# LogSumExp over rows: the second pass on another queue, the range check in two parts, two loads in quarters

## The chip, the cores and the metric

The kernel runs on one core of one Trainium2 chip. The metric is the device time of one execution in microseconds. Nine runs of the kernel before gave a median of 165.54 us, from 165.21 to 165.82.

## The reference

For every row of `x`, of shape 32 x 512 x 1024 in float32, the reference computes the logarithm of the sum of exponentials, made safe by the row's maximum:

```python
max_x = np.max(x, axis=-1, keepdims=True)
return (max_x.squeeze(-1) + np.log(np.sum(np.exp(x - max_x), axis=-1))).astype(np.float32)
```

The input is drawn from a standard normal distribution. That makes 16,384 rows of 4 KB, 67.11 MB to read and 64 KB to write.

## The kernel before

The 16,384 rows are laid over 128 partitions: partition p holds the 128 consecutive rows from 128 p on, so a row index `c` from 0 to 127 names one row on every partition. Neighbouring partitions lie 512 KB apart in memory. The kernel gambles that no maximum is needed: it takes exp, sum and logarithm directly, checks at the end that all sums were in a safe range, and only if one was not does it run a second pass that subtracts the maximum.

**The first pass.** Seventeen loads, listed as strings in `loads` (L42), go through the SyncE (SP) queue into `ring`, a buffer of 48 rows per partition that is filled round and round. A load moves between 16 rows and 1 row per partition; the sizes fall towards the end. The string says how the rows are then summed: `R8` is an exp over eight rows on ScalarE (L92) and one reduction on VectorE (L99); `A` is an exp on ScalarE whose own accumulator gives the sum (L90); `T` is an exp on ScalarE and then one VectorE instruction per row that adds the row's halves and accumulates (L104). The sums go to `sumexp`, one column per row index. The logarithm is taken in two parts: the first 104 columns in the middle of the stream (L119), the last 24 at the end (L121). Then SP writes `res` out (L122).

**The range check.** After the stream, VectorE clamps 127 columns of `sumexp` into 1e-15 to 1e15 (L127) and compares them with the originals, with an accumulated count of the unequal ones in `bad` (L131). The 128th row, the last to arrive, is treated apart: the maximum of the first 256 elements of its input is taken (L136) and compared with -34 (L137), and its sum itself enters the total. Three tiny matmuls add everything over the partitions into one number `count` in PSUM (L135, L140, L141), and `fine` is whether that number is below 1e15 (L143).

**The branch and the end.** `values_load` (L144) has SP, ScalarE and VectorE each load `fine` into a register and branch on it (L148). In the untaken case each engine brings its semaphores up to what the second pass would have made of them and jumps to the end. There SP waits for every semaphore that the program used, one or two at a time, and drains. All engines then meet at a barrier that GpSimd gathers and releases.

**What sets the order.** Each engine works its instructions in program order. A framework assigns the waits: every DMA takes the next of eight hardware semaphores in turn, and waits that the program declares unneeded are left out. The closing waits of SP name these semaphores in a list; the one of the output DMA stands first in the kernel before.

The second pass (L149 to L160) runs on SP for the loads and the store, on VectorE and ScalarE for the computation. With the given input it is not executed.

Of the kernel before, what the change touches and what calls it, by code (L numbers as in the profile page):

```python
# [9 lines left out]
LOW, HIGH = 1e-15, 1e15  # L10
LOG_LOW = -34.0


@with_exitstack
def kernel(
    ctx: ExitStack,
    tc: tile.TileContext,
    x: bass.AP,
    out: bass.AP,
):  # L20
    nc = tc.nc
    P = nc.NUM_PARTITIONS
    fp32 = mybir.dt.float32
    i32 = mybir.dt.int32
    AF = mybir.ActivationFunctionType
    AX = mybir.AxisListType
    ALU = mybir.AluOpType

    x_flat = x.flatten_outer_dims()
    n, d = x_flat.shape  # L30
    assert n % P == 0
    NC = n // P
    H = d // 2

    x_rows = x_flat.rearrange("(p c) d -> p c d", p=P)
    out_view = out.rearrange("a b -> (a b)").rearrange("(p c) -> p c", p=P)

    RING = 48
    loads = [  # L42
        "R8 R8", "R8 R8", "R8 R8", "R7 R6 A A", "R6 R5 A A A", "R5 R4 A", "R5 R4", "R5 T3",
        "R3 A A A", "R3 A", "R2 T2", "R3", "R1 A", "T2", "T1", "A", "A",
    ]
    loads = [[(op[0], int(op[1:] or 1)) for op in load.split()] for load in loads]
    assert sum(s for ops in loads for _, s in ops) == NC
    ENGINES = [mybir.EngineType.SP, mybir.EngineType.Activation, mybir.EngineType.DVE]
    EARLY = 104
    LAST = NC - 1  # L50

    big = ctx.enter_context(tc.tile_pool(name="big", bufs=1))
    stats = ctx.enter_context(tc.tile_pool(name="stats", bufs=1))
    psum = ctx.enter_context(tc.tile_pool(name="psum", bufs=1, space=bass.MemoryType.PSUM))

    ring = big.tile([P, RING, d], fp32, name="ring")
    sumexp = stats.tile([P, NC], fp32, name="sumexp")
    res = stats.tile([P, NC], fp32, name="res")
    clamped = stats.tile([P, NC], fp32, name="clamped")
    bad = stats.tile([P, 3], fp32, name="bad")  # L60
    fine = stats.tile([1, 1], i32, name="fine")
    far = stats.tile([P, 1], fp32, name="far")
    ones = stats.tile([P, 1], fp32, name="ones")
    last_exp = psum.tile([P, 1, d], fp32, name="last_exp")
    count = psum.tile([1, 1], fp32, name="count")

    nc.scalar.preload_act_table_set("natural_log_exp_and_others")  # L67
    nc.vector.memset(ones, 1.0)  # L68
    nc.vector.memset(far, 100 * HIGH)

    def load(p0, c0, size):
        return nc.sync.dma_start(out=ring[:, p0 : p0 + size, :], in_=x_rows[:, c0 : c0 + size, :])  # L72

    def without_wait(ins, group, reason):

        tc.declare_no_dep(ins.ins, group=group, reason=reason)

    c = 0
    p = 0
    for ops in loads:  # L80
        size = sum(s for _, s in ops)
        if p + size > RING:
            p = 0
        dma = load(p, c, size).ins
        for how, s in ops:
            v = ring[:, p : p + s, :]
            sums = sumexp[:, c : c + s]
            if how == "A":
                o = v if c < LAST else last_exp
                exp = nc.scalar.activation(out=o, in_=v, func=AF.Exp, accum_out=sums)  # L90
            else:
                exp = nc.scalar.activation(out=v, in_=v, func=AF.Exp)  # L92
            without_wait(exp, "loads", "the slot's earlier users came before this load")
            without_wait(exp, "exps", "the slot's earlier users came before this load")
            without_wait(exp, "sums", "the slot's earlier users came before this load")
            tc.add_to_no_dep_group("exps", exp.ins)
            added = []
            if how == "R":
                added = [nc.vector.reduce_sum(out=sums, in_=v, axis=AX.X)]  # L99
            elif how == "T":  # L100
                for r in range(s):
                    lo = ring[:, p + r, 0:H]
                    added.append(
                        nc.vector.scalar_tensor_tensor(  # L104
                            out=lo, in0=lo, scalar=1.0, in1=ring[:, p + r, H:d],
                            op0=ALU.mult, op1=ALU.add, accum_out=sums[:, r : r + 1],
                        )
                    )
            for add in added:
                tc.declare_no_dep(add.ins, dma, reason="ScalarE has waited for it")  # L110
                without_wait(add, "loads", "they came before this one")
            for add in added:
                tc.add_to_no_dep_group("sums", add.ins)
            c += s
            p += s
            last_row = v
        tc.add_to_no_dep_group("loads", dma)
        if c == EARLY + 14:
            nc.scalar.activation(out=res[:, 0:EARLY], in_=sumexp[:, 0:EARLY], func=AF.Ln)  # L119

    nc.scalar.activation(out=res[:, EARLY:NC], in_=sumexp[:, EARLY:NC], func=AF.Ln)  # L121
    nc.sync.dma_start(out=out_view, in_=res)  # L122

    nc.vector.tensor_scalar(  # L127
        out=clamped[:, 0:LAST], in0=sumexp[:, 0:LAST],
        scalar1=LOW, scalar2=HIGH, op0=ALU.max, op1=ALU.min,
    )  # L130
    nc.vector.scalar_tensor_tensor(  # L131
        out=clamped[:, 0:LAST], in0=clamped[:, 0:LAST], scalar=0.0, in1=sumexp[:, 0:LAST],
        op0=ALU.bypass, op1=ALU.not_equal, accum_out=bad[:, 0:1],
    )
    nc.tensor.matmul(count, lhsT=bad[:, 0:1], rhs=far, start=True, stop=False)  # L135
    nc.vector.reduce_max(out=bad[:, 2:3], in_=last_row[:, 0, 0 : d // 4], axis=AX.X)  # L136
    nc.vector.tensor_scalar(  # L137
        out=bad[:, 1:2], in0=bad[:, 2:3], scalar1=LOG_LOW, scalar2=None, op0=ALU.is_lt
    )
    nc.tensor.matmul(count, lhsT=bad[:, 1:2], rhs=far, start=False, stop=False)  # L140
    nc.tensor.matmul(count, lhsT=sumexp[:, LAST:NC], rhs=ones, start=False, stop=True)  # L141

    nc.vector.tensor_scalar(out=fine, in0=count, scalar1=HIGH, scalar2=None, op0=ALU.is_lt)  # L143
    all_fine = nc.values_load(  # L144
        fine[0:1, 0:1], engines=ENGINES, min_val=0, max_val=1,
        skip_runtime_bounds_check_because="a truth value",
    )
    with tc.If(all_fine < 1, preferred_fallthrough_block=False):  # L148
        for c0 in range(0, NC, RING):  # L149
            s = min(RING, NC - c0)  # L150
            v = ring[:, 0:s, :]
            neg = clamped[:, c0 : c0 + s]
            load(0, c0, s)
            nc.vector.tensor_reduce(out=neg, in_=v, op=ALU.max, axis=AX.X, negate=True)
            nc.vector.tensor_add(out=v, in0=v, in1=neg[:, :, None].to_broadcast([P, s, d]))
            nc.scalar.activation(out=v, in_=v, func=AF.Exp)
            nc.vector.reduce_sum(out=sumexp[:, c0 : c0 + s], in_=v, axis=AX.X)
        nc.scalar.activation(out=res, in_=sumexp, func=AF.Ln)
        nc.vector.tensor_sub(out=res, in0=res, in1=clamped)
        nc.sync.dma_start(out=out_view, in_=res)  # L160


# [28 lines left out]
```

## Time and profile before

| what | value |
|---|---|
| median of nine runs | 165.54 us (165.21 to 165.82) |
| profiled execution, its own time | 165.34 us |
| its span | 163.5 us |
| VectorE busy | 122.2 us, 75% |
| ScalarE busy | 116.7 us, 71% |
| TensorE busy | 0.4 us |
| load queue, share of the 16 DMA engines | 95.9% |
| mean transfer rate over the span | 411 GB/s |

The span is the time from the first to the last instruction of the program; the execution's own time is 1.8 us longer. PE is the TensorE matmul, PEld its weight load, DVE VectorE, ACT ScalarE, POOL GpSimd and SP SyncE; a q behind a name means the sequencer or queue of that engine. Branches, semaphore waits and register loads are not counted as busy and appear only when a source line is asked for.

### The profile page before, as it was taken

The numbers are of one execution on the slowest core, as the hardware profiler recorded it, in microseconds if no ns is written. First come the engines' busy times: TensorE is split into PE (matmuls) and PEld (weight loads), VectorE is DVE, ScalarE is ACT, GpSimd is POOL, SyncE is SP. The second block draws the span as 40 slices with busy tenths as digits, with TensorE's granted clock in tenths as the row PEclk, the third lists the DMA queues.
The fourth block names the chain that finished last, engine by engine and source line by source line (L and its number), as shares of the span: only waits on it lengthen the run. The fifth ranks groups of instructions, "written<-read, shape, count | busy, mean of one in ns | idle before, by whom it ended". The sixth has DMA issues, their size and how long they took to land.

```text
span 163.5 us, 205 instructions
## 1 busy us (share of the span) xinstructions
PE 0.4 (0%) x6; PEld 0.2 (0%) x6; DVE 122.2 (75%) x44; ACT 116.7 (71%) x53; POOL 0.2 (0%) x4
## 2 busy tenths in 40 slices
PE   0000000000000000000000000000000000000001
PEld 0000000000000000000000000000000000000000
DVE  0000000699968999499999995999998999979893
ACT  3000039990699708995499839999969599999992
POOL 0000000000000000000000000000000000000000
DMA  7979988998997998899999999999999999999970
GB/s 256 497 337 449 513 385 385 513 417 353 513 449 321 513 482 376 361 481 481 449 435 407 435 391 431 411 409 433 433 449 425 411 445 419 421 427 417 411 281 20
DMA packets 2594, 67.19 MB, mean 411 GB/s; under 512 B 288, under 2 KB 416, under 8 KB 800
## 3 DMA queue, kind: packets, MB, share of 16 engines
q1 hardware_dynamic: 2592, 67.18, 95.9%
q14 instruction: 2, 0.02, 0.0%
HBM read 67.11 MB, written 0.07 MB: 411 GB/s over the span
## 4 chain that ended last, share of the span: by engine, by line
DMA 63%; DVE 22%; ACT 12%; issue 1%; SPq 0%; PE 0%; DVEq 0%
DMA ring<-in_x_dram 63%; DVE sumexp L99 20%; ACT ring L92 12%; DVE ring L104 1%; SPq L72 0%; DVE bad L136 0%; DVE clamped L127 0%; PE count L140 0%; DVE bad L137 0%; DVE clamped L131 0%; DVE fine L143 0%; PE count L141 0%; DVEq L127 0%
## 5 line engine op out<-in xcount | busy, mean ns | idle before, releaser
L99 DVE TENSOR_REDUCE sumexp<-ring 128x8 f32<-128x8192 f32 (+7 forms) x20 | 116.2, 5854 | 37.7 <-ACT ring L92 37.6
L92 ACT ACTIVATE ring<-ring 128x8192 f32<-128x8192 f32 (+7 forms) x24 | 101.7, 4283 | 43.1 <-DMA ring<-in_x_dram 43.1
L90 ACT ACTIVATE ring<-ring 128x1024 f32<-128x1024 f32 x12 | 12.5, 1039 | 0.0
L104 DVE SCALAR_TENSOR_TENSOR ring<-ring 128x512 f32<-128x512 f32 x8 | 5.1, 684 | 0.0
L90 ACT ACTIVATION_READ_ACCUMULATOR ring<-ring 128x1 f32 x12 | 2.2, 186 | 0.0
L67 ACT ACT_TABLE_LOAD x1 | 1.3, 1283 | 0.7 <-PEq L175 0.7
L90 ACT ACTIVATE last_exp<-ring 128x1024 f32<-128x1024 f32 x1 | 1.0, 1014 | 0.0
L68 DVE MEMSET ones<- 128x1 f32 x1 | 0.1, 59 | 0.8 <-PEq L175 0.8
L104 DVE DVE_READ_ACCUMULATOR ring<-ring 128x1 f32 x8 | 0.7, 82 | 0.0
L135 PE MATMUL count<-far,bad 128*1 128x1 f32 x2 | 0.2, 164 | 160.3 <-DVE clamped L131 160.3
L136 DVE TENSOR_REDUCE bad<-ring 128x1 f32<-128x256 f32 x1 | 0.4, 415 | 0.0
L143 DVE TENSOR_SCALAR fine<-count 1x1 int32<-1x1 f32 x1 | 0.1, 147 | 0.3 <-PE count L141 0.3
L131 DVE SCALAR_TENSOR_TENSOR clamped<-clamped,sumexp 128x127 f32<-128x127 f32 x1 | 0.3, 291 | 0.0
L127 DVE TENSOR_SCALAR clamped<-sumexp 128x127 f32<-128x127 f32 x1 | 0.2, 227 | 0.1
L135 PEld LDWEIGHTS count<-far,bad 128*1 128x1 f32 x2 | 0.1, 80 | 160.3 <-DVE clamped L131 160.3
L119 ACT ACTIVATE res<-sumexp 128x104 f32<-128x104 f32 x1 | 0.3, 273 | 0.0
L121 ACT ACTIVATE res<-sumexp 128x24 f32<-128x24 f32 x1 | 0.2, 223 | 0.0
L140 PE MATMUL count<-far,bad 128*1 128x1 f32 x2 | 0.2, 164 | 0.3 <-DVE bad L137 0.3
L141 PE MATMUL count<-ones,sumexp 128*1 128x1 f32 x2 | 0.2, 164 | 0.0
L90 ACT ACTIVATION_READ_ACCUMULATOR last_exp<-ring 128x1 f32 x1 | 0.2, 186 | 0.0
L137 DVE TENSOR_SCALAR bad<-bad 128x1 f32<-128x1 f32 x1 | 0.2, 154 | 0.0
L141 PEld LDWEIGHTS count<-ones,sumexp 128*1 128x1 f32 x2 | 0.1, 81 | 0.0
(7 smaller groups left out, 0.6 us busy)
## 6 DMA issues: line engine op xcount, KB each, us to landing
ring<-in_x_dram SPq DMA_DIRECT2D x1, 7680.0 KB, 32.5
ring<-in_x_dram SPq DMA_DIRECT2D x1, 7168.0 KB, 30.1
ring<-in_x_dram SPq DMA_DIRECT2D x1, 5120.0 KB, 31.4
ring<-in_x_dram SPq DMA_DIRECT2D x1, 4608.0 KB, 33.7
ring<-in_x_dram SPq DMA_DIRECT2D x1, 4096.0 KB, 29.3
ring<-in_x_dram SPq DMA_DIRECT2D x2, 2048.0 KB, 32.7
ring<-in_x_dram SPq DMA_DIRECT2D x1, 3072.0 KB, 36.3
ring<-in_x_dram SPq DMA_DIRECT2D x2, 1024.0 KB, 38.8
```

The costliest lines, as they stand in the source:

```text
L67: nc.scalar.preload_act_table_set("natural_log_exp_and_others")
L90: exp = nc.scalar.activation(out=o, in_=v, func=AF.Exp, accum_out=sums)
L92: exp = nc.scalar.activation(out=v, in_=v, func=AF.Exp)
L99: added = [nc.vector.reduce_sum(out=sums, in_=v, axis=AX.X)]
L104: nc.vector.scalar_tensor_tensor(out=lo, in0=lo, scalar=1.0, in1=ring[:, p + r, H:d], op0=ALU.mult, op1=ALU.add, accum_out=sums[:, r : r + 1],
L119: nc.scalar.activation(out=res[:, 0:EARLY], in_=sumexp[:, 0:EARLY], func=AF.Ln)
L121: nc.scalar.activation(out=res[:, EARLY:NC], in_=sumexp[:, EARLY:NC], func=AF.Ln)
L127: nc.vector.tensor_scalar(out=clamped[:, 0:LAST], in0=sumexp[:, 0:LAST], scalar1=LOW, scalar2=HIGH, op0=ALU.max, op1=ALU.min,)
L131: nc.vector.scalar_tensor_tensor(out=clamped[:, 0:LAST], in0=clamped[:, 0:LAST], scalar=0.0, in1=sumexp[:, 0:LAST], op0=ALU.bypass, op1=AL ...
L135: nc.tensor.matmul(count, lhsT=bad[:, 0:1], rhs=far, start=True, stop=False)
L136: nc.vector.reduce_max(out=bad[:, 2:3], in_=last_row[:, 0, 0 : d // 4], axis=AX.X)
L141: nc.tensor.matmul(count, lhsT=sumexp[:, LAST:NC], rhs=ones, start=False, stop=True)
```

## The change

The change has three parts.

First, SP no longer loads `fine` and does not branch; only ScalarE and VectorE do. The second pass is put into a critical section, in which the framework places no waits of its own and the program uses two semaphores, `landed` and `ready`. Its loads and its store are issued from the ScalarE queue.

Second, the range check becomes a function, `check`, called twice: for columns 0 to 117 after the load that ends at column 121, and for columns 118 to 126 at the end. In the built program the first call stands on VectorE ahead of the reduction of the three rows that begin at column 118. There is one more tiny matmul. The maximum of the last row is taken over the first 64 elements instead of 256.

Third, the two loads that begin at rows 32 and 48 are each issued as four DMAs of 32 partitions, every fourth partition in each, where one DMA moved 128. The number of load DMAs rises from 17 to 23, and with it the semaphore of the output DMA changes from the second to the eighth; in SP's closing list it then stands in the last wait.

```diff
-    ENGINES = [mybir.EngineType.SP, mybir.EngineType.Activation, mybir.EngineType.DVE]
+    ENGINES = [mybir.EngineType.Activation, mybir.EngineType.DVE]
     EARLY = 104
+    LATE = 118
...
     def load(p0, c0, size):
-        return nc.sync.dma_start(out=ring[:, p0 : p0 + size, :], in_=x_rows[:, c0 : c0 + size, :])
+        step = 4 if c0 in (32, 48) else 1
+        return [
+            nc.sync.dma_start(
+                out=ring[k::step, p0 : p0 + size, :], in_=x_rows[k::step, c0 : c0 + size, :]
+            ).ins
+            for k in range(step)
+        ]
...
+    def check(c0, c1, i):
+        nc.vector.tensor_scalar(
+            out=clamped[:, c0:c1], in0=sumexp[:, c0:c1],
+            scalar1=LOW, scalar2=HIGH, op0=ALU.max, op1=ALU.min,
+        )
+        nc.vector.scalar_tensor_tensor(
+            out=clamped[:, c0:c1], in0=clamped[:, c0:c1], scalar=0.0, in1=sumexp[:, c0:c1],
+            op0=ALU.bypass, op1=ALU.not_equal, accum_out=bad[:, i : i + 1],
+        )
+        nc.tensor.matmul(count, lhsT=bad[:, i : i + 1], rhs=far, start=i == 0, stop=False)
...
+        if c == LATE + 3:
+            check(0, LATE, 0)
...
-    nc.vector.reduce_max(out=bad[:, 2:3], in_=last_row[:, 0, 0 : d // 4], axis=AX.X)
+    check(LATE, LAST, 1)
+    nc.vector.reduce_max(out=bad[:, 3:4], in_=last_row[:, 0, 0 : d // 16], axis=AX.X)
...
     with tc.If(all_fine < 1, preferred_fallthrough_block=False):
-        for c0 in range(0, NC, RING):
-            s = min(RING, NC - c0)
...
-            load(0, c0, s)
...
+        with tc.tile_critical(sync_engine=mybir.EngineType.Activation):
+            with nc.semaphore("landed") as landed, nc.semaphore("ready") as ready:
...
+                    nc.scalar.dma_start(out=v, in_=x_rows[:, c0 : c0 + s, :]).then_inc(landed, 16)
...
+                nc.scalar.dma_start(out=out_view, in_=res).then_inc(landed, 16)
+                nc.scalar.wait_ge(landed, rows + 16)
```

## The prediction

> **What bounds the kernel now.** I read the DMA part of the page first, then the busy time by stage, then the timeline of the end, then the branch and barrier records that no busy figure counts.
>
> ```profile
> q1 hardware_dynamic: 2592, 67.18, 95.9%
> ...
> out_dram<-res SPq DMA_DIRECT2D x1, 64.0 KB, 1.5
> ```
>
> The load queue fills 95.9% of the 16 DMA engines' span. The busy time by stage (columns: stretch, its length, busy of PE, PEld, DVE, ACT, POOL with counts, PE clock, DMA share, GB/s):
>
> ```profile
> 1.70:41.50 39.80, 0.00 (x0) 0.00 (x0) 11.32 (x2) 14.26 (x3) 0.00 (x0) 1.00 1.01 431
> 41.50:79.90 38.40, 0.00 (x0) 0.00 (x0) 34.28 (x5) 27.90 (x4) 0.00 (x0) 1.00 1.01 437
> ...
> 141.00:158.40 17.40, 0.00 (x0) 0.00 (x0) 15.67 (x14) 17.13 (x17) 0.00 (x0) 1.00 0.99 411
> 158.40:163.50 5.10, 0.43 (x6) 0.22 (x6) 2.29 (x10) 2.17 (x5) 0.00 (x0) 1.00 0.07 20
> ```
>
> From 1.7 to 158.4 us the DMA share is 0.99 or more: the transfer is the bound, an edit of the compute before 158 us wins nothing and can only lose, by delaying a load; only the last 5.1 us are open. The packet records say the same: a 64 KB packet takes 2418 ns on every engine, start to end (16 x 65,536 B / 2418 ns = 433.7 GB/s). The timeline of the end:
>
> ```profile
> 152.38 0.08 DVE L104 DVE_READ_ACCUMULATOR ring<-ring 128x1 f32 x1
> 153.22 4.48 DVE L99 TENSOR_REDUCE sumexp<-ring 128x3 f32<-128x3072 f32 x2 [0.76 <-ACT ring L92]
> ...
> 159.64 0.23 DVE L127 TENSOR_SCALAR clamped<-sumexp 128x127 f32<-128x127 f32 x1
> 159.90 0.29 DVE L131 SCALAR_TENSOR_TENSOR clamped<-clamped,sumexp 128x127 f32<-128x127 f32 x1
> ...
> 160.12 0.41 DVE L136 TENSOR_REDUCE bad<-ring 128x1 f32<-128x256 f32 x1
> ...
> 160.57 0.15 DVE L137 TENSOR_SCALAR bad<-bad 128x1 f32<-128x1 f32 x1
> 160.62 0.35 SPq L122 DMA_DIRECT2D out_dram<-res  x1
> ...
> 161.05 0.15 DVE L143 TENSOR_SCALAR fine<-count 1x1 int32<-1x1 f32 x1 [0.33 <-PE count L141]
> ```
>
> Two paths run side by side: the output DMA, issued at 160.62 and landed at 162.17 (its last semaphore record), and the check on DVE and PE, whose truth value stands at 161.20. Then the branch (L144, L148) and the end (L186), with columns count, ns min/median/max, first and last start:
>
> ```profile
> L144 SPq TENSOR_LOAD <-fine x1: 463/463/463, 161.2 to 161.2; - x1
> ...
> L148 SPq EVENT_SEMAPHORE  x4: 17/17/17, 161.9 to 162.1; - x4
> L148 SPq COMPARE_BRANCH  x2: 38/44/49, 161.8 to 162.2; - x2
> ```
> ```profile
> L186 SPq EVENT_SEMAPHORE  x7: 17/28/28, 162.3 to 162.7; - x7
> L186 SPq DRAIN  x2: 7/7/7, 162.8 to 162.8; - x2
> L186 POOLq EVENT_SEMAPHORE  x2: 17/17/17, 162.9 to 163.0; - x2
> L186 ACTq DRAIN  x1: 93/93/93, 162.3 to 162.3; - x1
> L186 DVEq DRAIN  x1: 51/51/51, 162.6 to 162.6; - x1
> ```
>
> The reader is to see who comes last to the barrier: SP. It loads the truth value, branches, jumps at 162.16, begins its closing waits at 162.33 (the output has landed 0.16 us before), works off seven at about 0.066 us each, and drains at 162.85; GpSimd answers at 162.88, and 0.67 us later the span ends at 163.55 (163.5 on the page). The hundredths come from the same records of the trace, read one by one. DVE arrived at 162.63, ACT at 162.33.
>
> **The change, part by part.**
>
> *SP leaves the branch.* Its value load (0.46 us), two branch records and four semaphore waits go. After issuing the output at 160.62 to 160.97 it jumps (0.17 us, as its jump at 162.16 took) and stands at its closing waits near 161.2. Before, six of seven waits followed the landing, 6 x 0.066 = 0.39 us. Now the order of the list matters: each DMA takes the next of eight semaphores in turn. 17 loads and the output make the output the 18th, on the second semaphore, which the list names first. Six more DMAs make it the 24th, on the eighth, which the built program names in the last of six waits. The others pass by about 161.65, as they need only the branch's semaphore updates of ACT and DVE. So SP is released by the landing, 162.17, passes the last wait at 162.19 and its two drains by 162.31, instead of 162.85: 0.54 us earlier.
>
> *DVE must come too.* Its drain stood at 162.63, so alone SP would win only 0.2 us. What shortens DVE: L127 on 9 columns instead of 127. Its slope is (227 - 154) / 126 = 0.58 ns a column, from L127 and the one-column L137, so 118 columns save 0.07 us. L131: (684 - 291) / (512 - 127) = 1.02 ns, from L104 and L131, saving 0.12 us. The maximum over 64 instead of 256 columns, at the 1.05 ns a column of L99's eight-row reductions (8.64 us for 8192), saves 0.20 us. Sum 0.39 us: L137 ends at 160.33, `fine` stands at 160.81, DVE's drain at 162.24 and ACT's near 162.0. Limit: the last matmul (L141) needs ACT's last sum, at 160.34, and would start at 160.43; 0.1 us is left there, so the whole 0.39 counts. DVE (162.24 plus its 0.05) is then just ahead of SP (162.31). GpSimd answers at about 162.35 instead of 162.88: 0.53 us.
>
> *The check that is moved ahead* (118 columns) stands on DVE between L104 at 152.46 and the three-row reduction at 153.22, where the timeline shows 0.76 us idle. Like L127 it starts 0.19 us after the accumulator read (152.65), takes 0.22, then about 0.22 until the pipelined next instruction may start: 153.12, so it fits with 0.1 us left. Behind it are queued that reduction, the last row sums, and through them ACT's last logarithm. If the cover is gone the cost is at most its 0.6 us on DVE; ACT's logarithm waits for sums ready at 159.53 and starts at 160.37, so 0.84 us of cover remains on the output path, but the check path would lose it all. Value taken 0, bounds 0 to 0.6. Its extra PE matmul (0.16) falls in idle PE.
>
> *The second pass* is not executed (all values are in range); ACT and DVE still jump over its longer code. DVE's jump took 0.57 us (162.06 to 162.63), ACT's 0.41, over 15 and 7 instructions, SP's 0.17 over 9, so length does not set it; I take it unchanged, plus one 0.07 us wait on ACT, which has 0.3 us to spare. Bounds: -0.1 to +0.5 on DVE.
>
> *Two loads as four each.* SP issues six more DMAs, 0.38 to 0.43 us each (the first two in the trace), the first three while two loads are in flight, the others at 48 us with load 32 to 47 flying until 61.8: hidden by 13 us of queued transfer, after which SP next issues at 66.8. The fourth quarter at row 48 waits also for the load of rows 16 to 31, landed at 42.4: no wait. Behind each engine's share the records show a 9 ns semaphore packet and the next data packet 12 ns after it: 6 x 12 ns = 0.07 us on the DMA path, which is the bound. ACT waits for four semaphores, up to 0.15 us late at 61.8 and 79.9, hidden in the 13 us of queue.
>
> What no row shows is the rate of a transfer of 32 partitions, every fourth. Two rules of the Trainium skill speak against it. DMA: Bandwidth & Descriptors, section Latency and other measured facts: copies whose rows lie 2 MiB apart reach 164 GB/s where a 512 KiB pitch gives 207. A quarter's rows lie 4 x 512 KiB apart; by the rule its 16.25 MB would take 37.5 x 207 / 164 = 47.3 us, +9.9 us. SBUF — State Buffer, section Can I just issue two DMAs to hit both halves: only one transfer over all 128 partitions reaches all 16 ports. Against this stands the row: now, at a 512 KiB pitch, one core reads at 433 GB/s. By the first page's section on the descriptor swizzle, four neighbouring partitions share one engine, so the 16 engines already stand on rows four apart, 2 MiB, at each moment; and every fourth partition still touches all ports. If engines keep these partitions the rate is the row's. If the 32 rows are cut into consecutive pairs, engines 0 and 4 meet on one port: at most double, +37.5 us. Taken: 0; bounds 0 to +37.5.
>
> **The sum.** -0.53 + 0.07 = -0.46 us. The profiled execution is 165.34 us around a span of 163.55, so 164.88 by its own time. It lies 0.20 us below the median of the runs, 165.54; taken from that median the sum gives 165.08, and I say 165.1.
>
> **The rivals.** (a) *DVE takes SP's place at the barrier.* DVE arrives only 0.02 us ahead of SP in my sum. If its jump grows by 0.3 us with the longer block, or the early check isn't covered, the barrier moves only 0.1 to 0.25 us: 165.36. For: the drain at 162.6. Against: three engines' jumps show no relation to length. (b) *The quarters lose rate*, slower than before: 175 by the pitch rule, up to 203 by port pairing. It decides early: 0.46 us in 37.5 is 1.2%, a 64 KB packet of 2448 ns instead of 2418; +0.33 us net needs 2.1%. Against: the swizzle argument. For: nothing in this trace moves 32 partitions. (c) *The semaphore order does nothing*, since the output lands later than thought or the drains wait elsewhere: SP keeps six waits (0.39 us) after the landing and wins only the 0.16 us by which it was late for it, less the 0.07: 165.45.
>
> **How the numbers follow.** A measurement of this kernel can tell 0.2%, 0.33 us, from no change. Main case 0.64 (164.85 to 165.3); (a) 0.16; (b) 0.13; (c) 0.07. Range 164.7 to 165.6 takes in main, (a) and (c), with the ends for spread between runs, and leaves (b) out. Faster: 0.64 less a little that falls short, 0.63; same: (a), (c) and that little, 0.24; slower 0.13.
>
> **What would show it.** SP at its closing waits before 161.7 and its last one at the landing; DVE's drain near 162.24; GpSimd's answer near 162.35, span near 163.1. The DMA share by stage at 0.99 or more between 41 and 80 us with the load of row 48 landed near 80. The idle before the three-row reduction nearly filled, its start still at 153.2. I am wrong if packets of the quarters run above 2450 ns, or DVE's drain stays at 162.6.

## The result, and the profile after

| | before | after |
|---|---|---|
| median, run side by side | 165.43 us (29 runs) | 164.84 us (9 runs, 164.73 to 165.07) |
| ratio after / before, 95% interval | | 0.9962 [0.9953, 0.9971] |
| profiled execution, its own time | 165.34 us | 165.03 us |
| its span | 163.55 us | 163.24 us |

The kernel is 0.59 us faster by the medians, 0.38% by the ratio. Forecast were 165.1 us, in a range from 164.7 to 165.6, with a chance of 0.63 for faster.

The stream first. The page's DMA part and the busy time by stage of the kernel after (columns: stretch, its length, busy of PE, PEld, DVE, ACT, POOL, PE clock, DMA share, GB/s):

```profile
q1 hardware_dynamic: 2688, 67.18, 96.1%
```
```profile
1.70:41.50 39.80, 0.00 (x0) 0.00 (x0) 11.35 (x2) 14.26 (x3) 0.00 (x0) 1.00 1.02 435
41.50:79.90 38.40, 0.00 (x0) 0.00 (x0) 34.21 (x5) 27.90 (x4) 0.00 (x0) 1.00 1.00 434
79.90:141.00 61.10, 0.00 (x0) 0.00 (x0) 58.37 (x13) 54.09 (x26) 0.00 (x0) 1.00 0.99 426
141.00:158.40 17.40, 0.19 (x2) 0.09 (x2) 16.19 (x17) 17.13 (x17) 0.00 (x0) 1.00 0.98 410
158.40:163.20 4.80, 0.43 (x6) 0.22 (x6) 2.16 (x12) 2.40 (x6) 0.00 (x0) 1.00 0.07 21
```

The 96 further packets are the six further DMAs, one semaphore packet for each of 16 engines. The second stage is the one with the quarters: DMA share 1.00, 434 GB/s. Their 64 KB packets take 2418 ns in the median, the same as those of whole loads. The load of row 48 is complete at 80.15 us, against 79.94 before; in a second profile of the kernel after it is complete at 79.96. So the quarters kept their rate.

The timeline, with the check that was moved ahead and then the end:

```profile
152.60 0.08 DVE L125 DVE_READ_ACCUMULATOR ring<-ring 128x1 f32 x1
152.72 0.22 DVE L89 TENSOR_SCALAR clamped<-sumexp 128x118 f32<-128x118 f32 x1
152.98 0.28 DVE L93 SCALAR_TENSOR_TENSOR clamped<-clamped,sumexp 128x118 f32<-128x118 f32 x1
...
153.45 3.35 DVE L120 TENSOR_REDUCE sumexp<-ring 128x3 f32<-128x3072 f32 x1 [0.18 <-ACT ring L113]
...
159.86 0.17 DVE L89 TENSOR_SCALAR clamped<-sumexp 128x9 f32<-128x9 f32 x1
160.07 0.17 DVE L93 SCALAR_TENSOR_TENSOR clamped<-clamped,sumexp 128x9 f32<-128x9 f32 x1
...
160.18 0.22 DVE L152 TENSOR_REDUCE bad<-ring 128x1 f32<-128x64 f32 x1
...
160.85 0.35 SPq L147 DMA_DIRECT2D out_dram<-res  x1
160.92 0.15 DVE L158 TENSOR_SCALAR fine<-count 1x1 int32<-1x1 f32 x1 [0.33 <-PE count L157]
```

The early check fits into the idle time before the three-row reduction: 0.18 us of the 0.76 are left, and what that reduction waits for is still ScalarE. At the end the two check instructions and the maximum are 0.17, 0.17 and 0.22 us long instead of 0.23, 0.29 and 0.41.

The load of `fine` (L159) and the closing waits with their barrier (L223), by count, ns min/median/max, first and last start:

```profile
L159 ACTq TENSOR_LOAD <-fine x1: 464/464/464, 161.1 to 161.1; - x1
L159 DVEq TENSOR_LOAD <-fine x1: 542/542/542, 161.1 to 161.1; - x1
```
```profile
L223 SPq EVENT_SEMAPHORE  x7: 17/28/438, 161.3 to 162.7; - x7
L223 SPq DRAIN  x3: 7/7/7, 162.5 to 162.8; - x3
L223 ACTq DRAIN  x2: 8/8/8, 162.3 to 162.8; - x2
L223 DVEq DRAIN  x2: 10/30/50, 162.5 to 162.8; - x2
L223 POOLq EVENT_SEMAPHORE  x2: 17/17/17, 162.6 to 162.6; - x2
```

SP loads no truth value any more. It stands at its closing waits at 161.25, not at 162.33, and there it waits: 438 ns for DVE's update after the branch, the longest of the row, and 247 ns in the next record for ScalarE's, to 162.15. Before, the longest took 28 ns, because everything had happened already. The output lands at 162.40, SP's last wait starts at 162.41, its second drain at 162.53, DVE's drain at 162.48, GpSimd answers at 162.57.

These absolute times hide part of the gain. In this execution the last load landed at 159.40, in the profile of before at 159.17. Such shifts come and go between executions of one kernel: the second profile of the kernel after has 159.21. The distance that the change can act on is the one from the last load's landing to GpSimd's answer, called the tail from here on: 3.71 us before, 3.17 and 3.19 us in the two profiles after. That is -0.53 us.

### The profile page after: what moved, and what is told of

The parts are those of the page before. It is cut to its first block, busy times and chain, and to the rows that moved or that the text cites. A ratio compares the mean times of both kernels' runs of the same rounds, so it can differ in the third digit from the quotient of the medians.

```text
span 163.2 us, 216 instructions
## 1 busy us (share of the span) xinstructions
PE 0.6 (0%) x8; PEld 0.3 (0%) x8; DVE 122.4 (75%) x47; ACT 116.7 (72%) x53; POOL 0.2 (0%) x4
## 4 chain that ended last, share of the span: by engine, by line
DMA 64%; DVE 22%; ACT 12%; issue 0%; SPq 0%; PE 0%; DVEq 0%
DMA ring<-in_x_dram 64%; DVE sumexp L120 21%; ACT ring L113 12%; DVE ring L125 1%; SPq L77 0%; PE count L156 0%; DVE clamped L89 0%; DVE bad L152 0%; DVE bad L153 0%; DVE clamped L93 0%; DVE fine L158 0%; PE count L157 0%; DVEq L89 0%
## 5 line engine op out<-in xcount | busy, mean ns | idle before, releaser
L93 DVE SCALAR_TENSOR_TENSOR clamped<-clamped,sumexp 128x118 f32<-128x118 f32 (+1 forms) x2 | 0.5, 226 | 0.1
```

The lines of the kernel that those rows point to most:

```text
L93: nc.vector.scalar_tensor_tensor(out=clamped[:, c0:c1], in0=clamped[:, c0:c1], scalar=0.0, in1=sumexp[:, c0:c1], op0=ALU.bypass, op1=ALU.n ...
```

## The experiments

The theory is that three things reach the end together, the output's landing, SP behind it and DVE with the check, so that each part alone wins little. The rivals are (b) and (c) of the prediction, that the quarters cost time or that the order of the closing waits does nothing, and a third, that one part does everything. The three parts are SP out of the branch (S), the check in two (C) and the two loads in quarters (Q). All eight combinations were run:

| parts | kernel | tail, us | median less that of before beside it, us | ratio, 95% |
|---|---|---|---|---|
| none | before | 3.71 | | |
| C | e4 | 3.56 | -0.10 | 0.9988 [0.9979, 0.9997] |
| Q | e3 | 3.72 | -0.09 | 0.9996 [0.9988, 1.0005] |
| S | e9 | 3.55 | -0.12 | 0.9995 [0.9986, 1.0004] |
| C, Q | e5 | 3.54 | -0.22 | 0.9987 [0.9978, 0.9995] |
| S, C | e1 | 3.39 | -0.36 | 0.9975 [0.9964, 0.9986] |
| S, Q | e2 | 3.50 | -0.21 | 0.9987 [0.9978, 0.9996] |
| S, C, Q | after | 3.17 | -0.59 | 0.9962 [0.9953, 0.9971] |
| S, C, Q | after again (e0) | 3.19 | -0.63 | 0.9968 [0.9957, 0.9980] |

The ratio is taken over the runs and not from the two medians, so it can differ from the difference beside it by up to 0.1 us. Its interval is some 0.15 us to either side, so the medians alone would not settle what a single part wins. The tails are finer: two profiles of the kernel after agree to 0.02 us, though every other kernel has only one. Tail and median move together within 0.11 us. The parts alone win 0.15, nothing and 0.16 us of tail, sum 0.30; together 0.53.

**e1: the loads whole again.** The output DMA is then on the second semaphore, and SP names it in the second of six closing waits.

```diff
-        step = 4 if c0 in (32, 48) else 1
+        step = 1
```

> The changed kernel with every load as one DMA again; the output then takes the second semaphore, which stands in the second of SP's six closing waits. Theory (the order of the closing waits is worth its waits, the quarters cost 0.07 us): four waits of 0.066 us follow the landing instead of none, +0.26 - 0.07, so 165.0 us. Rival 1 (the profile's later last load, +0.23 us, is the price of the quarters): +0.26 - 0.23, so 164.85 us. Rival 2 (the order of the waits is worth nothing): 164.77 us or less, with GpSimd's answer no further behind the last load's landing than the 3.17 us of the changed kernel.

Measured: 165.11 us, 0.9975 [0.9964, 0.9986]. SP's closing records:

```profile
L223 SPq EVENT_SEMAPHORE  x6: 17/28/1110, 161.4 to 162.8; - x6
L223 SPq DRAIN  x2: 7/7/7, 162.9 to 162.9; - x2
L223 DVEq DRAIN  x1: 49/49/49, 162.7 to 162.7; - x1
L223 POOLq EVENT_SEMAPHORE  x1: 17/17/17, 163.0 to 163.0; - x1
```

SP now stands 1110 ns at the output's wait, to 162.60 (landing 162.58), and has four waits behind it, from 162.63 to 162.82, before it drains at 162.94. In the kernel after, the others are done at 162.15, and only the last one is left behind the landing. DVE is at 162.69 and does not matter. Against the two profiles of the kernel after, the position of one semaphore in the list is worth 0.20 to 0.22 us of tail, and 0.23 to 0.27 us of median when each is taken against the kernel before beside it.

**e2: the whole check at the end again, over 256 elements of the last row.**

```diff
-        if c == LATE + 3:
-            check(0, LATE, 0)
...
-    check(LATE, LAST, 1)
-    nc.vector.reduce_max(out=bad[:, 3:4], in_=last_row[:, 0, 0 : d // 16], axis=AX.X)
+    check(0, LAST, 0)
+    nc.vector.reduce_max(out=bad[:, 3:4], in_=last_row[:, 0, 0 : d // 4], axis=AX.X)
```

> The changed kernel with the whole range check at the end and the maximum over 256 elements again. Theory (DVE stands right behind SP at the barrier): DVE's drain moves 0.39 us later and takes SP's place; GpSimd's answer stands 0.37 us later, 165.2 us. Rival (SP alone holds the barrier, the check is hidden): 164.84 us.

Measured: 165.26 us, 0.9987 [0.9978, 0.9996], tail 3.50. Its closing records:

```profile
L221 SPq EVENT_SEMAPHORE  x7: 17/28/776, 161.1 to 162.8; - x7
L221 SPq DRAIN  x3: 7/7/7, 162.4 to 162.9; - x3
L221 DVEq DRAIN  x2: 10/30/50, 162.6 to 162.9; - x2
L221 POOLq EVENT_SEMAPHORE  x2: 17/17/17, 162.7 to 162.8; - x2
```

SP drains at 162.46, DVE only at 162.62, and GpSimd answers 0.08 us after DVE. DVE has taken SP's place at the barrier, the mechanism of rival (a).

**e3: the kernel before with the two loads in quarters, and nothing else.**

```diff
-    def load(p0, c0, size):
-        return nc.sync.dma_start(out=ring[:, p0 : p0 + size, :], in_=x_rows[:, c0 : c0 + size, :])
+    def load(p0, c0, size, first=True):
+        step = 4 if first and c0 in (32, 48) else 1
+        return [
+            nc.sync.dma_start(
+                out=ring[k::step, p0 : p0 + size, :], in_=x_rows[k::step, c0 : c0 + size, :]
+            ).ins
+            for k in range(step)
+        ]
...
```

> The kernel before with only the two loads in quarters; the output stands in the last of SP's seven closing waits. Theory (SP comes to its waits 0.16 us after the landing, so their order is worth nothing while SP branches): 165.43 + 0.07 = 165.5 us, up to 165.66 if the quarters cost 0.23. Rival (the order alone wins): 165.43 - 0.39 + 0.07 = 165.1 us.

Measured: 165.38 us, 0.9996 [0.9988, 1.0005], tail 3.72. The quarters by themselves neither win nor lose anything that these runs can tell, and the new place of the output's semaphore is worthless as long as SP reaches its closing waits after the landing.

**e4: the kernel before with the check in two parts, and nothing else.**

```diff
...
+        if c == LATE + 3:
+            check(0, LATE, 0)
...
-    nc.vector.tensor_scalar(
-        out=clamped[:, 0:LAST], in0=sumexp[:, 0:LAST],
...
-    nc.vector.reduce_max(out=bad[:, 2:3], in_=last_row[:, 0, 0 : d // 4], axis=AX.X)
+    check(LATE, LAST, 1)
+    nc.vector.reduce_max(out=bad[:, 3:4], in_=last_row[:, 0, 0 : d // 16], axis=AX.X)
...
```

> The kernel before with only the range check in two parts and the maximum over 64 elements; SP still branches, the output still stands in the first closing wait. Theory: truth value, branch and SP's arrival are 0.39 us earlier, so SP stands before the landing and has six waits, 0.39 us, behind it: GpSimd's answer 0.15 us earlier, 165.3 us. Rival (the check is the whole of the gain): 164.85 us.

Measured: 165.37 us, 0.9988 [0.9979, 0.9997], tail 3.56. `fine` is loaded earlier, SP reaches the closing waits 0.02 us behind the landing instead of 0.16, and that is the whole gain of 0.15 us: seven waits still follow.

**e0: the kernel after once more, beside e5, e6 and e8.**

> The changed kernel unchanged, for a second profile and as the measure for the other runs of this call. If the quarters delay the stream, its last load lands again near 159.40 us, 0.23 us behind the kernel before; if that was chance, near 159.24. 164.84 us either way, within 0.15.

Measured: 164.86 us (7 runs), 0.9968 [0.9957, 0.9980], tail 3.19. The last load landed at 159.21.

**e5: check and quarters, but SP still branches.** Against the kernel after:

```diff
-    ENGINES = [mybir.EngineType.Activation, mybir.EngineType.DVE]
+    ENGINES = [mybir.EngineType.SP, mybir.EngineType.Activation, mybir.EngineType.DVE]
...
-        with tc.tile_critical(sync_engine=mybir.EngineType.Activation):
...
+            load(0, c0, s, first=False)
...
```

> The kernel before with the check in two parts and the quarters, but the second pass and the branch still on SP too. Theory: SP comes to its closing waits at 161.95 us, works off seven by 162.34, 0.1 us after the landing: 0.39 us earlier than before, 165.05 us, so that taking SP out of the branch is worth only 0.1 to 0.2 us once the two other parts are in. Rival (SP's leaving the branch is what wins): 165.3 us or more, as with the check alone.

Measured: 165.27 us, 0.9987 [0.9978, 0.9995], tail 3.54. This was a miss: I had expected the early check to let SP come early enough for the semaphore's place to count. The load of the truth value and SP's closing records show why it did not:

```profile
L157 ACTq TENSOR_LOAD <-fine x1: 464/464/464, 160.9 to 160.9; - x1
...
L157 SPq TENSOR_LOAD <-fine x1: 484/484/484, 161.1 to 161.1; - x1
```
```profile
L199 SPq EVENT_SEMAPHORE  x7: 17/28/28, 162.2 to 162.6; - x7
L199 SPq DRAIN  x2: 7/7/7, 162.7 to 162.7; - x2
```

`fine` stands at 160.93, and ScalarE and DVE load it then. SP loads it at 161.09, because the output issue (160.69, 0.35 us) stands ahead of it on the same queue. So SP's branch ends at 162.24, 0.01 us behind the landing at 162.23, no closing wait exceeds 28 ns, and seven of them follow. From here on a faster check cannot bring SP further forward; the work ahead of the branch is SP's own. In the kernel before it was different. There SP's issue was over at 160.97, and ScalarE and VectorE load the truth value at the same time as SP, at 161.23 to 161.24:

```profile
L144 ACTq TENSOR_LOAD <-fine x1: 468/468/468, 161.2 to 161.2; - x1
L144 DVEq TENSOR_LOAD <-fine x1: 546/546/546, 161.2 to 161.2; - x1
```

So there the check set the time of SP's load; the issue on SP's queue becomes the limit only once the check is earlier.

**e10: e5 with the output issued from ScalarE.** If that reading holds, taking the issue off SP must let SP branch earlier.

```diff
-    nc.sync.dma_start(out=out_view, in_=res)
+    nc.scalar.dma_start(out=out_view, in_=res)
```

> The kernel before with the check in two parts and the quarters, SP still in the branch, and the first pass's output issued from the ScalarE queue. Theory (SP's load of the truth value stands behind its issue of the output, 0.35 us, and so came at 161.09 instead of 160.93 however early the check): without that issue SP loads at 160.93, jumps at about 161.9, has six waits behind it at the landing, and GpSimd answers 3.25 us after the last load's landing instead of 3.54: 165.0 us. Rival (what holds SP is the branch itself with its four waits and jump): 3.45 us or more, 165.2 us.

Measured: 165.06 us, 0.9975 [0.9965, 0.9986], tail 3.38: between the two values expected. SP loads the truth value at 160.95, and now ScalarE loads it late, at 161.12, behind its own issue. SP's closing records:

```profile
L199 SPq EVENT_SEMAPHORE  x7: 17/28/28, 162.1 to 162.5; - x7
L199 SPq DRAIN  x2: 7/7/7, 162.5 to 162.6; - x2
```

They begin at 162.09, 0.15 us earlier than in e5 and ahead of the landing (162.28), but the seven waits of 0.066 us are a chain of their own that ends at 162.50, after it. SP's load and its arrival both moved forward by 0.14 to 0.15 us, as the reading of e5 has it; the size I expected was too large: SP would have to arrive 6 x 0.066 = 0.40 us ahead of the landing for the place of the semaphore to count in full. Of the kernels tried, only those in which it leaves the branch do that.

**e9: SP out of the branch, and nothing else.** The two edits of e1 and e2 together on the kernel after.

```diff
-        step = 4 if c0 in (32, 48) else 1
+        step = 1
...
-        if c == LATE + 3:
-            check(0, LATE, 0)
...
-    check(LATE, LAST, 1)
-    nc.vector.reduce_max(out=bad[:, 3:4], in_=last_row[:, 0, 0 : d // 16], axis=AX.X)
+    check(0, LAST, 0)
+    nc.vector.reduce_max(out=bad[:, 3:4], in_=last_row[:, 0, 0 : d // 4], axis=AX.X)
```

> The kernel before with only the second pass in its own section and SP out of the branch; loads as before, whole check at the end. Theory (DVE stands behind SP): SP has four waits after the landing and would be done 0.28 us earlier, but DVE's drain stays where it was, 0.2 us ahead of the old answer: GpSimd's answer 3.5 us after the last load's landing instead of 3.71, as with the check put back in the changed kernel (3.50); 165.3 us. Rival (SP's leaving is the gain): 164.95 us, 3.2 us after the landing.

Measured: 165.35 us, 0.9995 [0.9986, 1.0004], tail 3.55. The closing records:

```profile
L221 SPq EVENT_SEMAPHORE  x6: 17/28/1111, 161.6 to 163.0; - x6
L221 SPq DRAIN  x2: 7/7/7, 163.0 to 163.1; - x2
...
L221 DVEq DRAIN  x1: 49/49/49, 163.2 to 163.2; - x1
```

SP drains at 163.09 and DVE at 163.19 (the last load landed at 159.72 here). Both limits stand behind the output's landing: the four waits, and DVE. Lifting one of them leaves the other.

**e11: the check of the last row's input left out.** The low side of the last row's range goes unexamined in this kernel: no maximum, no comparison, one matmul less.

```diff
     check(LATE, LAST, 1)
-    nc.vector.reduce_max(out=bad[:, 3:4], in_=last_row[:, 0, 0 : d // 16], axis=AX.X)
-    nc.vector.tensor_scalar(
-        out=bad[:, 2:3], in0=bad[:, 3:4], scalar1=LOG_LOW, scalar2=None, op0=ALU.is_lt
-    )
-    nc.tensor.matmul(count, lhsT=bad[:, 2:3], rhs=far, start=False, stop=False)
```

> The changed kernel without the maximum of the last row and its comparison and matmul: the low side of the last row's range is left unchecked. Theory (SP, released by the output's landing, now ends the kernel, and the truth value waits for ScalarE's last sum): GpSimd's answer stays 3.15 us behind the last load's landing, 164.85 us. Rival (DVE's check is the bound): 0.3 us earlier, 164.55 us.

Measured: 164.84 us, 0.9958 [0.9944, 0.9972], tail 3.16. The closing records:

```profile
L218 SPq DRAIN  x3: 7/7/7, 162.4 to 162.7; - x3
...
L218 DVEq DRAIN  x2: 10/30/51, 162.4 to 162.8; - x2
```

That is the time and the tail of the kernel after, with work left out. DVE comes only 0.06 us earlier, counted from the last landing, since the truth value still waits for ScalarE's last sum; its drain ends at 162.43, ahead of the end of SP's second drain at 162.49. With DVE out of the way the tail stays, so a shorter check alone wins nothing more: the landing of the output, and the one wait and two drains of SP behind it, are a bound.

**e7: the quarters as blocks of 32 neighbouring partitions.** This measures what the prediction left as its largest unknown, the rate of a transfer of 32 partitions.

```diff
+    def part(k, step):
+        return slice(k * P // step, (k + 1) * P // step)
...
-                out=ring[k::step, p0 : p0 + size, :], in_=x_rows[k::step, c0 : c0 + size, :]
+                out=ring[part(k, step), p0 : p0 + size, :], in_=x_rows[part(k, step), c0 : c0 + size, :]
```

> The changed kernel with the quarters taken as blocks of 32 neighbouring partitions instead of every fourth. Theory (a DMA engine's rate is bound to the SBUF port that the partition belongs to, and 32 neighbouring partitions touch half of the ports): the two loads take up to twice their 37.5 us, up to 202 us, packets of 64 KB near 4800 ns. Rival (any 32 partitions go at full rate, so the stride was never needed): 164.85 us, packets of 2418 ns. [...]

Measured: 206.88 us (2 runs), 1.2500 [1.2476, 1.2523], so +41.4 us, some 5 us more than the limit expected. First the stage with the quarters in e7, then the row of DMA issues for the four quarters at row 48 (KB each, median us to landing), e7 ahead of the kernel after:

```profile
41.50:121.50 80.00, 0.00 (x0) 0.00 (x0) 40.70 (x5) 27.90 (x4) 0.00 (x0) 1.00 0.99 209
```
```profile
ring<-in_x_dram SPq DMA_DIRECT2D x4, 1920.0 KB, 59.8
```
```profile
ring<-in_x_dram SPq DMA_DIRECT2D x4, 1920.0 KB, 24.9
```

The engines are as full as ever (0.99) and move 209 GB/s; a 64 KB packet takes 5111 ns instead of 2418, 2.11 times as long. The tail is 3.23, so everything that was lost was lost in the stream. The number is near that of the page SBUF — State Buffer of the Trainium skill, section Door 1: The DMA port swizzle, by which partitions 0 to 31 reach half of the 16 ports and some 218 GB/s. But the two kernels also show that the count of partitions is not what matters: 32 partitions four apart keep 2418 ns. That the ports are the cause is not shown: between the two kernels the distance of the rows in memory changes too, and no run separates it from the place in the buffer.

**e8: the same two loads cut by rows, all 128 partitions in each part.**

```diff
+        cuts = [size * k // step for k in range(step + 1)]
...
-                out=ring[k::step, p0 : p0 + size, :], in_=x_rows[k::step, c0 : c0 + size, :]
+                out=ring[:, p0 + a : p0 + b, :], in_=x_rows[:, c0 + a : c0 + b, :]
...
-            for k in range(step)
+            for a, b in zip(cuts, cuts[1:])
```

> The changed kernel with the same two loads cut into four by rows instead of partitions: the same number of DMAs and the same semaphores, 128 partitions each, packets of 12 and 16 KB instead of 60 and 64. By the packet records of the kernel before (611 ns for 16 KB, 461 for 12 KB, 2418 for 64) these 37.5 us take 1.1 to 1.9% longer: +0.4 to +0.7 us, 165.3 to 165.5 us. Rival (the cut is free either way): 164.84 us.

Measured: 165.38 us, 0.9995 [0.9986, 1.0003], tail 3.18. The tail keeps the whole gain, since the number of DMAs and so the output's semaphore is the same; the stream gives it back: the last load lands at 159.76 instead of 159.21 in the kernel after beside it, 0.37 us of which arise within the two loads, and the median is 0.52 us later. Taking every fourth partition keeps packets of 60 and 64 KB, cutting by rows leaves 12 and 16 KB.

**e6: the first two loads in quarters instead of the third and fourth.** The idea was that the stream's first microsecond, in which the 16 engines start one after the other, might come from the 128 partitions of the first load.

```diff
-        step = 4 if c0 in (32, 48) else 1
+        step = 4 if c0 in (0, 16) else 1
```

> The changed kernel with the loads of rows 0 and 16 in quarters instead of those of rows 32 and 48. In the trace the 16 DMA engines take up their first packets one after the other over 1.0 us, from 1.75 to 2.75. If that ramp comes from the 128 partitions of the first DMA, a first DMA of 32 starts all within 0.3 us and the last load lands up to 0.5 us earlier: 164.3 to 164.8 us. Rival (the ramp doesn't depend on it, or the rate is shared so that the total counts): 164.84 us.

Measured: 165.38 us, 0.9993 [0.9984, 1.0001], a miss. The first packets of the 16 engines start between 2.05 and 3.22 us, with whole loads between 1.75 and 2.75: the ramp is as long and begins 0.3 us later. The last load lands at 159.51. The tail is 3.34: DVE drains at 162.76, behind SP (162.64). Of the 0.17 us by which DVE is later than in the kernel after, counted from the last landing, 0.12 stand ahead of its load of the truth value, where it has one more semaphore wait before the maximum, and 0.05 are that load itself, 0.60 us instead of 0.54.

## Why the prediction was right

**SP, -0.54 us: right.** Taking off the 0.23 us by which this execution's stream ended later, SP's second drain is at 162.30 (forecast 162.31), and GpSimd's answer at 162.34 (forecast 162.35). One step in it was mis-sized without effect: the other waits were to pass by about 161.65, and with the same 0.23 taken off they passed at 161.92, released by ScalarE's update after its branch. That is still 0.24 us ahead of the landing. e1 shows that the place of the output's semaphore is part of the gain, e9 that SP's absence alone is not enough.

**DVE, -0.39 us: right, a little over-sized.** `fine` is loaded 1.69 us after the last landing instead of 2.06, -0.37; the three short instructions took 0.172, 0.169 and 0.219 us for 0.159, 0.171 and 0.215. DVE's drain, less the same 0.23, is at 162.25 (forecast 162.24). e2 shows that the rest of the gain hangs on it.

**The early check at nothing: right.** It ran under the cover that was named, with 0.18 us of idle time left. **The longer second pass at nothing on DVE: right.** DVE's jump took 0.57 us again. ScalarE's wait and branch together cost it more than forecast (drain at 162.10 instead of 162.0, less the 0.23), still ahead of the landing.

**The quarters at their old rate: right,** and the two rules that spoke against it did not decide. The pitch rule of DMA: Bandwidth & Descriptors, which that page measured on copies between tensors in memory, would have had the stage at 164/207 of its rate (+9.8 us, not +9.9); it ran at 434 GB/s. e7 turns that rule's order round: the slow blocks are rows 512 KiB apart, the fast quarters rows 2 MiB apart. The section of SBUF — State Buffer, by which only one transfer over all 128 partitions reaches all 16 ports, did not hold back the quarters; e7's 209 GB/s fits half the ports for neighbouring partitions. The reason given, that each engine keeps its partitions, is not shown: the records at hand do not name the engine of a packet. SP's issues of the quarters were under-sized, 0.47 to 0.83 us each in the kernel after for 0.38 to 0.43, but they were hidden as forecast. The upper price of rival (b), +37.5 us, is near what e7 lost, +41.4, but by a cut that the change does not make.

**+0.07 us for the semaphore packets of six more DMAs: not seen.** This is the one term of the sum that no run confirms. From the landing of row 16's load to that of row 48's, the two loads took 37.50 to 37.76 us in the seven profiles of kernels that have them in quarters (after, e0, e2, e3, e5, e10, e11), and 37.51 to 38.11 in the four with whole loads only (before, e1, e4, e9). The last load landed between 159.16 and 159.40 in the same seven, and between 159.17 and 159.72 in the four. Single slow packets, 2840 or 2958 ns for instance instead of 2418, occur in both groups, and with such a spread a profile cannot resolve 0.07. In the medians e3 is not slower than before. The interval of e3, up to +0.08 us, does not exclude the term.

**The sum.** -0.53 without the 0.07, from the 165.43 us that the kernel before had in the runs beside the kernel after (the nine shown ahead had 165.54), gives 164.90; the median is 164.84. So 0.11 of the 0.24 us between forecast and result is the base, 0.07 the quarters' term, and 0.06 is left, less than the medians can tell.

**The rivals.** (a) is the true mechanism of e2 and e9. In the change itself DVE was to be 0.02 us ahead of SP, and it came out as a tie: DVE's drain ends 0.01 us ahead of SP's second one in the first profile (162.53 against 162.54) and 0.02 us behind it in the second (162.36 against 162.34). So the change lies at the edge of (a), at no visible cost; that the two came out level, and DVE no later, was in part luck, as the bounds given for DVE's jump alone, -0.1 to +0.5 us, were far wider than 0.02. (c) falls by e1: in the kernel after, one wait follows the landing. What I had not seen is what holds SP once the check is earlier: the issue of the output on its own queue, ahead of the load of the truth value (e5, e10). In the kernel before it was the truth value itself.

## What to carry to other kernels

When several engines meet at the end, list for each of them when it arrives and what it still has to work off there; a part that brings one forward wins only up to the next, so parts that win 0.15, 0.00 and 0.16 us alone can win 0.53 together. An engine that issues the last DMA should have nothing to do behind it but wait, and of its closing waits the one that is satisfied last should stand last. In these runs a load could be cut into DMAs of fewer partitions at no visible cost when every part took every fourth partition and kept the packet's size (434 GB/s); cut into blocks of neighbouring partitions it ran at half the rate (209 GB/s). Another stride was not tried.

## What was unexpected of the hardware

- **Which 32 partitions.** 64 KB packets took 2418 ns for every fourth partition and 5111 ns for 32 neighbouring ones (e7), with the DMA share at 0.99 or more in both. Whether the place in the buffer or the distance of the rows in memory is the cause was not separated.
- **The start of the stream.** The 16 engines begin over 0.9 to 1.2 us, whether the first DMA has 128 partitions or 32; with 32, every fourth, they begin 0.3 us later (e6). SP's issue of that first DMA takes 0.54 us instead of 0.38, which is half of it; the rest was not tried.
- **ScalarE's branch.** One of its steps takes 0.40 us, but not the same in every kernel. In the kernel after, in e2, e3, e5 and e11 it is the first step after the comparison (161.62 to 162.02 in the kernel after) and the jump takes 0.16; in the kernel before, e1, e4 and e9 the jump takes 0.40 and the first step 0.08; in e10 neither is slow (0.08 and 0.16). Apart from e10 this divides like quartered and whole loads; the cause was not tested, and ScalarE came before SP or DVE to the barrier in all of them.
